# Indexer queries and keys projected features first, with the rotary product on features

## The chip, the cores and the metric

The kernel runs on one core of one Trainium2 chip. The metric is the device time of one execution in microseconds (us). Three runs of the kernel before took 337.05, 338.77 and 338.71 us; the median is 338.71 us.

## What is computed

One encoder layer over 512 tokens with 1024 features. After an RMS norm, one projection feeds two head groups. Group A is attention over 128 keys per query, chosen by a small indexer; group B is latent attention over all admissible keys. Both outputs are gated, concatenated, projected and added to the input. The change touches the indexer's inputs only:

```python
q_i = q_i.reshape(B, S, IDX_HEADS, IDX_DIM)                    # 8 heads of 64
q_i = concatenate([rope(q_i[..., :32], pos), q_i[..., 32:]], -1)
k_i = k_i[:, :, None, :]                                       # one head of 64
k_i = concatenate([rope(k_i[..., :32], pos), k_i[..., 32:]], -1)[:, :, 0, :]
...
rel   = relu(einsum('bqhd,bsd->bqhs', q_i, k_i))
score = einsum('bqhs,bqh->bqs', rel, w_i) * idx_scale          # then mask, top 128
# rope on 32 features: [x1*cos - x2*sin, x2*cos + x1*sin], x1 the first 16, x2 the last 16
```

The first 128 queries need no choice (they have at most 128 keys), so the indexer runs for the token tiles 1, 2 and 3 (384 queries).

## The kernel before

Nearly all products are made of three matmuls on values split into a high and a low part (`mm3`, `mm3w`: high by high, high by low, low by high). Weights arrive in chunks of 128 rows by DMA into `wst`; ScalarE (ACT) rounds a chunk to its high part `wh`, and GpSimd (POOL), or for some chunks VectorE (DVE), subtracts to get the low part `wl`. Chunks 0 to 7 are those of `q_i`, 8 to 15 of `c_kv`, 16 to 23 of `c_q` (whose low parts DVE makes). There are three `wst` buffers for chunks from 8 on, and nine each of `wh` and `wl`, so a chunk waits until TensorE (PE) is through with the chunk nine places ahead.

The order on PE is the order in which the program is written; the helpers `stream` and `weave` interleave several accumulations, and `later` puts a piece of work off by a stated time. The other engines take the order that the scheduler chose when the kernel was built, strictly one after another. PSUM has eight banks in four tags: `mm` 3, `tr` 2, `sc` 2, `pv` 1.

The stretch in question lies from about 15 to 58 us:

- The "small" projection (104 columns: key rope of group B, indexer key, indexer weights) accumulates with features on partitions. Its last eight matmuls use the low weights `swl`. Then `use_small` copies it out, transposes it by token (four 104-wide transposes into `tr`), rotates the key on DVE, and transposes it back to features (`turn2`), where ACT rounds it to KIH and DVE subtracts to KIL.
- The queries: for each of three token tiles, eight steps of three matmuls with 512 columns (72 matmuls), tokens on partitions, in the banks `mm`, `mm`, `pv`. The three accumulations start 1.99 steps apart. `use_qi` copies and rotates (DVE multiplies by tables `cs32` broadcast over heads), then four transposes per tile bring features on partitions, ACT writes the high parts into `QI[0]` and `QI[1]`, and DVE the low parts beside them.
- The `c_kv` projection follows: two accumulations (banks `mm` and `pv`) of eight steps each, the second starting three steps after the first. After nine steps the indexer is woven in: for each tile (3, 2, 1) and head, two matmuls into the banks `sc` and `tr` in turn, a ReLU on ACT in place, and one multiply-add on DVE into `acc`. With two banks a tag, head 4 needs the bank that head 0 used, once DVE has added head 0. The `c_q` projection is woven between the later heads.
- On POOL, between the `wl` subtractions, lie the tables `tb` and `ta` for the rotary products of the other heads.

Of the kernel before, what the change touches and what calls it, by code (L numbers as in the profile page):

```python
# [15 lines left out]
S = 512  # L16
# [9 lines left out]
def constants():  # L26

    pos = np.arange(S, dtype=np.float32)

    def table(d):  # L30
        half = d // 2
        freqs = np.power(10000.0, -np.arange(half) * 2.0 / d).astype(np.float32)
        ang = (pos[:, None] * freqs[None, :]).astype(np.float64)
        c, s = np.cos(ang), np.sin(ang)
        t = np.stack([np.concatenate([c, c], 1), np.concatenate([-s, s], 1)], 1)
        return t.reshape(NT, 128, 2, d).transpose(1, 2, 0, 3).reshape(128, -1).astype(np.float32)

    q = np.arange(128)
    mask = np.where((q[None, :] // 64) <= (q[:, None] // 64), 0.0, NEG).astype(np.float32)
    wide = np.concatenate([np.zeros((128, 384), np.float32), mask], 1)  # L40
    return np.ascontiguousarray(
        np.concatenate([table(64), table(32), np.eye(128, dtype=np.float32), wide], 1))

# [17 lines left out]
KEEP_UP = 4  # L63

WARM = 11

TK = (2, 5, 5, 13, 12, 6)
I0, I1, I2 = 9, 5, 20
# [20 lines left out]
def layer(ctx: ExitStack, tc: tile.TileContext, x, norm_gain, w_in, a_q_norm, a_k_norm, b_q_latent,  # L89
# [14 lines left out]
    def tmp(shape=(128, 512)):  # L104
        return sb("tmp", shape)
# [5 lines left out]
    def psum(tag):  # L111
        return PS.tile([128, 512], F32, name=tag, tag=tag, bufs=BANKS[tag])

    def f32(ap):
        return ap.bitcast(F32)
# [4 lines left out]
    def tok(t):  # L120
        return slice(t * 128, t * 128 + 128)
# [11 lines left out]
    def transpose(o, i, idn):  # L133
        nc.tensor.transpose(o, i, idn)  # L134
        clock[0] += 107.0

    def later(ns, fn, served=False):

        waiting.append((clock[0] + ns, len(waiting), fn, served))
# [72 lines left out]
        nc.sync.dma_start(xin[t // 2][:, t % 2], xv[:, t])  # L212
    for a in range(0, 8, 4):
        ks = slice(a, a + 4)
        nc.sync.dma_start(wst[:, ks, 0:32], wv[:, ks, 3272:3304])
        nc.sync.dma_start(wst[:, ks, 32:104], wv[:, ks, 2560:2632])


    nc.gpsimd.memset(ident, 1.0)
# [12 lines left out]
    def after(v, u):  # L232

        tc.add_manual_dep(v.ins, u.ins.name, mybir.DependencyInfo(
            mybir.DependencyClass.NoSync, mybir.DependencyReason.DATA), reason="order")
# [9 lines left out]
    for _ in range(WARM):  # L245
        matmul(warm, zero[:, 0:128].bitcast(F32R), zero.bitcast(F32R), True, True)

    wake = P.tile([128, 1], F32, name="wake")
    wake_ = nc.scalar.activation(wake, epsc, AF.Square)
    for d in (nc.scalar.dma_start(grow[0:8], norm_gain.rearrange("(k p) -> k p", p=128)),  # L250
# [4 lines left out]
    def first(ins, m):  # L255

        for c in copies[used[0] + 1 + m:]:
            after(c, ins)
# [61 lines left out]
    def tok_jobs(name, nk, lh, ll, n, tiles, use, c=0, mm3=mm3):  # L320

        def job(t):
            def step(a, k):
                h, l = wt(name, k)
                mm3(a[:, :n], lh(k)[:, tok(t)], ll(k)[:, tok(t)], h[:, c:c + n], l[:, c:c + n], k == 0, k == nk - 1)
            return nk, step, lambda a: use(t, a)

        return [job(t) for t in tiles]
# [33 lines left out]
    def xh(k):  # L362
        return XH[k // 4][:, k % 4]
# [69 lines left out]
    def halves(ap):  # L433
        return ap.rearrange("p h (s d) -> p h s d", s=2)
# [9 lines left out]
    def split(h, l, p):  # L444
        return nc.scalar.copy(h, p), nc.vector.tensor_tensor(l, p, f32(h), op=OP.subtract)  # L445


    sm = P.tile([128, NT, 104], F32, name="sm")
    KIH = sb("z3", (128, S), F32R, "kih")
    KIL = sb("z3", (128, S), F32R, "kil")  # L450

    QSUM = []

    def use_small(_, a):
        st = tmp()
        first(nc.scalar.copy(st[:104], a[:104]), KEEP_SMALL)

        def turn():
            p = psum("tr")
            for t in range(NT):  # L460
                transpose(p[:, t * 104:t * 104 + 104], st[:104, tok(t)], ident[:104, :104])
            nc.scalar.copy(sm.rearrange("p t c -> p (t c)"), p[:, :416])
            p3 = p[:, :416].rearrange("p (t c) -> p t c", t=NT)

            kid = tmp((128, NT, 128))
            k4 = kid.rearrange("p t (u d) -> p t u d", u=2)
            m = tmp((128, NT, 32))
            for u in range(2):
                nc.scalar.copy(k4[:, :, u, 32:64], p3[:, :, 64:96])
            src = p3[:, :, 32:64]  # L470
            nc.vector.tensor_tensor(halves(m), halves(src)[:, :, ::-1, :], halves(cs32[:, 1]), op=OP.mult)
            nc.vector.tensor_tensor(src, src, cs32[:, 0], op=OP.mult)
            for u in range(2):
                nc.vector.tensor_tensor(k4[:, :, u, 0:32], src, m, op=OP.add)
            nc.scalar.activation(sm[:, :, 96:104], sm[:, :, 96:104], AF.Copy, scale=512 ** -0.5)

            def turn2():
                p = psum("tr")
                for t in range(NT):
                    transpose(p[:, tok(t)], kid[:, t], ident)  # L480
                kil = split(KIH, KIL, p)[1]
                if len(QSUM) == 3:
                    after(kil, QSUM[2])
            later(LAG_KI, turn2)
        later(LAG_SMALL, turn)

    dve = [None]
# [19 lines left out]

    def lat_kv(_, a):
        latent(a, 11, ckv, ckvs, "pt2")

    x_turn(0)
    gp = psum("sc")
# [21 lines left out]
    for a in range(0, 8, 4):  # L534
        ks = slice(a, a + 4)
        SWD.append(nc.vector.tensor_tensor(SWL[:, ks], wst[:, ks], f32(SWH[:, ks]), op=OP.subtract))
    qi_ = stream(tok_jobs("q_i", 8, xh, xl, 512, [1, 2, 3], lambda t, a: use_qi(t, a), mm3=mm3w), 3, ("mm", "mm", "pv"), 1.99)
    for i, ks in enumerate(((0,), (1,), (2, 3), (4, 5), (6, 7))):
        for k in ks:
            small_step(1, k)  # L540
        run(take(qi_, i // 2 + 1))
        if i == 0:
            xa, xd = [[f[hf, k] for hf in range(2) for k in range(8)] for f in (XA, XD)]
            chain(wake_, SQ[0], SQ[1], SQ[2], gains_, *xa[:2], SQ[3], SWA[0], *xa[2:8], copies[0],
                  *xa[8:10], copies[1], *xa[10:12], copies[2], *xa[12:], copies[3], copies[4])
            chain(TTR[0], TTR[1], *SCL[0], *SCL[1], TTR[2], TTR[3], xd[0], *SCL[2], *xd[1:], dsubs[0], *SWD)
            chain(*POW[0], *POW[1], *POW[2], *POW[3], *SCL[3], SWA[1], *subs[:3])
        if i == 2:
            nc.sync.dma_start(cs32, cst[:, 512:768])
    for k in range(8):  # L550
        matmul(sm_acc[:104], SWL[:, k], xh(k), False, k == 7)
    nc.sync.dma_start(wide, cst[:, 896:1408])
# [8 lines left out]
    HALF = slice(0, 64), slice(64, 128)  # L561
    QI = [sb("qk8", (128, 4, 384), F32R, f"qi{u}") for u in range(2)]

    def use_qi(t, a):
        q = tmp()
        q3 = q.rearrange("p (h d) -> p h d", h=8)
        m = tmp((128, 8, 32))
        a3 = a.rearrange("p (h d) -> p h d", h=8)
        first(nc.scalar.copy(q3[:, :, 32:64], a3[:, :, 32:64]), KEEP_QI)
        rope_mul(a3[:, :, 0:32], m, a3[:, :, 0:32], cs32, t, 8, 32)  # L570
        QSUM.append(nc.vector.tensor_tensor(q3[:, :, 0:32], a3[:, :, 0:32], m, op=OP.add))

        def turn():
            p = psum("tr" if t == 1 else "sc")
            for h in range(4):
                transpose(p[:, tok(h)], q[:, tok(h)], ident)
            p3 = p.rearrange("p (h c) -> p h c", h=4)
            for u in range(2):
                nc.scalar.copy(QI[u][HALF[u], :, tok(t - 1)], p3[HALF[u]])
            for u in range(2):  # L580
                a, b = QI[u][HALF[u], :, tok(t - 1)], QI[u][HALF[1 - u], :, tok(t - 1)]
                nc.vector.tensor_tensor(b, p3[HALF[u]], f32(a), op=OP.subtract)
        later(LAG_QI, turn)

    run(qi_)
    with tc.issue_after(subs[-1].ins):
# [6 lines left out]
    def index():  # L593
        for t in (3, 2, 1):
            n = (t + 1) * 128
            acc = masks[t] = ACC[t]
            for h in range(8):
                u = h % 2
                p = psum(("sc", "tr")[h % 2])
                matmul(p[:, :n], QI[u][:, h // 2, tok(t - 1)], KIH[:, :n], True, False)  # L600
                matmul(p[:, :n], QI[u][:, h // 2, tok(t - 1)], KIL[:, :n], False, True)
                r = p
                nc.scalar.activation(r[:, :n], p[:, :n], AF.Relu)
                w = sm[:, t, 96 + h:97 + h]
                if h == 0:
                    nc.vector.scalar_tensor_tensor(acc, r[:, :n], w, wide[:, 512 - n:], op0=OP.mult, op1=OP.add)
                else:
                    dve[0] = nc.vector.scalar_tensor_tensor(acc, r[:, :n], w, acc, op0=OP.mult, op1=OP.add).ins
                yield 1
# [69 lines left out]

    sq = tmp((128, 2, NT, 32))  # L680
    ssr = small(4)
    src = sm[:, :, 0:32]
    nc.scalar.activation(sq[:, 0], src, AF.Square)
    nc.vector.tensor_reduce(ssr, sq[:, 0], axis=AX.X, op=OP.add)
    nc.vector.tensor_scalar(kb, ssr, 1.0 / 96, EPS, op0=OP.mult, op1=OP.add)
# [382 lines left out]
```

## Time and profile before

| what | value |
|---|---|
| runs | 337.05, 338.77, 338.71 us |
| median | 338.71 us |
| profiled execution: span from the first to the last instruction | 335.4 us |
| the median less that span | 3.3 us |
| granted TensorE clock, mean | 0.999 |
| mean DMA traffic over the span | 104 GB/s |

The page gives no time for the profiled execution other than its span; the 3.3 us are what lies around it (and what one execution differs from another). The page lists busy time by engine, then the chain of work that ended last, then groups of instructions. A busy PE is not PE at its peak, since the ends of matmuls are modelled: rows of PE overlap, and what counts is the distance between the starts of two neighbours. A row of the timeline gives start, duration, engine, line, operation, output and inputs, shapes, and a count where several were merged; in brackets stands the idle time before it and what ended it.

### The profile page before, as it was taken

The page shows a single profiled execution, that of the slowest core. Times are in us where ns is not written, and L with a number is a line of the kernel's source. Part 1 is how long each engine was busy: PE and PEld are TensorE (multiplying, and loading weights), DVE is VectorE, ACT ScalarE, POOL GpSimd, SP SyncE. Part 2 cuts the span into 40 slices and gives each one's busy share as a digit, 9 for nine tenths or more (in the row PEclk, how much of TensorE's full clock was granted, in tenths as well). Part 3 has the DMA queues.
Part 4 walks back from the last instruction along what each step waited for, and adds up shares of the span by engine and source line. Part 5 has one row for each costly group of instructions (what it writes and reads, how often), then busy time and mean ns, then how long its engine had stood idle before and what let it go on. Part 6 is the DMA issues. An engine that isn't in the chain of part 4 may idle for free.

```text
span 335.4 us, 5485 instructions
## 1 busy us (share of the span) xinstructions
PE 327.5 (98%) x1691; PEld 274.0 (82%) x1691; DVE 261.3 (78%) x630; ACT 214.8 (64%) x530; POOL 183.7 (55%) x203
## 2 busy tenths in 40 slices
PE   7799999999999999999999999999999999999995
PEld 5788887888898988888888888888788788888884
DVE  4863779769999595778899989777997776878466
ACT  3935659583666676878876889434526988978210
POOL 3756443366899996235714579538734535745100
PEclk9999999999999999999999999999999999999999
DMA  7932343233133325014200354307977324410006
GB/s 254 306 108 51 108 119 117 63 104 95 34 103 94 94 70 150 1 34 122 70 30 1 73 144 136 91 0 183 241 173 225 96 74 141 127 64 1 2 0 250
DMA packets 28663, 34.77 MB, mean 104 GB/s; under 512 B 5325, under 2 KB 16730, under 8 KB 28634
## 3 DMA queue, kind: packets, MB, share of 16 engines
q1 hardware_dynamic: 25856, 32.45, 33.8%
q10 hardware_dynamic: 2778, 1.97, 2.2%
q8 instruction: 13, 0.21, 0.3%
q14 instruction: 16, 0.13, 0.1%
HBM read 27.07 MB, written 2.10 MB: 87 GB/s over the span
## 4 chain that ended last, share of the span: by engine, by line
PE 91%; DVE 3%; DMA 2%; issue 1%; ACT 1%; POOL 1%; SPq 0%; DVEq 0%; POOLq 0%
PE mm L130 53%; PE sc L130 12%; PE pv L130 11%; PE tr L134 6%; PE tr L130 5%; DMA xin<-in_x 2%; PE mm L134 2%; DVE ob L1023 2%; PE sc L134 1%; PE pv L134 1%; POOL tmp L838 0%; SPq L212 0%; DVE mal L841 0%; DVE z L762 0%; DVE xin L383 0%
## 5 line engine op out<-in xcount | busy, mean ns | idle before, releaser
L300 POOL TENSOR_TENSOR wl<-wst,wh 128x512 fp32r<-128x512 f32 (+2 forms) x80 | 100.6, 1267 | 47.8 <-ACT wh L297 38.6
L297 ACT CAST wh<-wst 128x512 fp32r<-128x512 f32 (+2 forms) x89 | 50.7, 587 | 23.5 <-DMA wst<-in_w_in 12.3
L130 PE MATMUL mm<-wh,xh 128*128 128x512 f32 x112 | 47.0, 419 | 0.0
L130 PE MATMUL mm<-wl,xh 128*128 128x512 f32 x112 | 44.4, 396 | 0.0
L130 PE MATMUL mm<-wh,xl 128*128 128x512 f32 x112 | 44.3, 395 | 0.0
L764 ACT ACTIVATE z<-z,sml 128x256 f32<-128x256 f32 (+2 forms) x64 | 35.9, 561 | 10.0 <-DVE sml L762 9.2
L793 POOL TENSOR_SCALAR z<-z,sml 128x512 f32<-128x512 f32 (+2 forms) x32 | 18.0, 564 | 42.4 <-DVE sml L789 32.8
L227 POOL TENSOR_TENSOR sml<-sml,nhalf 128x4 f32<-128x4 f32 (+2 forms) x28 | 31.8, 1141 | 14.9 <-ACT sml L916 13.7
L130 PE MATMUL mm<-xh,wh 128*128 128x512 f32 x88 | 36.6, 416 | 0.0
L130 PE MATMUL mm<-xl,wh 128*128 128x512 f32 x88 | 34.8, 395 | 0.0
L130 PE MATMUL mm<-xh,wl 128*128 128x512 f32 x88 | 34.7, 394 | 0.0
L619 DVE MAX8 m<-acc 128x8 f32<-128x512 f32 (+2 forms) x48 | 26.4, 553 | 0.0
L620 DVE MATCH_REPLACE8 acc<-m,acc 128x512 f32<-128x512 f32 (+2 forms) x48 | 26.0, 543 | 0.0
L130 PEld LDWEIGHTS mm<-wh,xl 128*128 128x128 f32 x112 | 21.1, 188 | 4.8
L130 PEld LDWEIGHTS mm<-wl,xh 128*128 128x128 f32 x112 | 21.2, 189 | 3.4 <-POOL wl L300 0.4
L130 PEld LDWEIGHTS mm<-wh,xh 128*128 128x128 f32 x112 | 21.1, 189 | 3.0 <-issue 0.2
L445 DVE TENSOR_TENSOR pl<-tr,ph 128x512 fp32r<-128x512 f32 (+1 forms) x32 | 17.6, 548 | 4.7 <-ACT ph L445 4.7
L762 DVE CUSTOM_DVE_ANT_0 z<-sc,wide,nqb 128x512 f32<-128x512 f32 (+3 forms) x32 | 17.3, 542 | 4.3 <-PE sc L130 4.0
L445 ACT CAST ph<-tr 128x512 fp32r<-128x512 f32 (+1 forms) x32 | 15.1, 473 | 8.5 <-PE tr L134 8.1
L130 PE MATMUL sc<-kl,bhl 96*128 96x512 f32 (+3 forms) x96 | 20.0, 320 | 0.0
L130 PEld LDWEIGHTS mm<-xh,wl 128*128 128x128 f32 x88 | 16.5, 188 | 3.9
L130 PEld LDWEIGHTS sc<-kl,bhl 96*128 96x128 f32 x96 | 16.7, 189 | 3.0
(248 smaller groups left out, 879.2 us busy)
## 6 DMA issues: line engine op xcount, KB each, us to landing
wst<-in_w_in SPq DMA_DIRECT2D x48, 256.0 KB, 2.7
wst<-in_w_out SPq DMA_DIRECT2D x16, 256.0 KB, 2.8
xin<-in_x SPq DMA_DIRECT2D x4, 512.0 KB, 5.5
ob<-in_x SPq DMA_DIRECT2D x8, 256.0 KB, 3.5
wst<-in_w_in SPq DMA_DIRECT2D x8, 192.0 KB, 2.4
wst<-in_w_uq SPq DMA_DIRECT2D x6, 192.0 KB, 2.5
wst<-in_w_in SPq DMA_DIRECT2D x8, 128.0 KB, 2.2
wst<-in_w_ukv SPq DMA_DIRECT2D x4, 256.0 KB, 2.9
```

What stands on the lines that cost most here:

```text
L130: nc.tensor.matmul(o, l, r, start=start, stop=stop)
L134: nc.tensor.transpose(o, i, idn)
L227: return nc.gpsimd.tensor_tensor(dst, src, nhalf[:, :src.shape[-1]], op=OP.pow)
L297: copies.append(nc.scalar.copy(h, st))
L300: i = E(eng).tensor_tensor(l, st, f32(h), op=OP.subtract)
L445: return nc.scalar.copy(h, p), nc.vector.tensor_tensor(l, p, f32(h), op=OP.subtract)
L619: nc.vector.max(m, masks[t])
L620: MR.append(nc.vector.match_replace(masks[t], m, masks[t], -3e38))
L762: m = nc.vector.tensor_tensor_reduce(z, sc[:, :n], mask(t), nq(h, t), 3e38, OP.add, OP.min, r[:, i:i + 1])
L764: e = nc.scalar.activation(z, z, AF.Exp, bias=r[:, i:i + 1], scale=-1.0, accum_out=r[:, 2 + i:3 + i])
L793: nc.gpsimd.tensor_scalar(z, z, w, 0.0, op0=OP.mult, op1=OP.add)
L1023: ADD[name, c, t] = nc.vector.tensor_tensor(o, p[:, :n], o, op=OP.add)
```

## The change

The queries are now projected with features on partitions: four groups of 128 features (two heads each), the weight chunk as the stationary operand and the 384 tokens of tiles 1 to 3 as the moving one. That is 32 steps of three matmuls with 384 columns (96 matmuls), in the banks `mm`, `mm`, `pv`, `sc`, again 1.99 steps apart. The small projection's columns are put in another order, so that the indexer key lies on partitions 0 to 63. For each group, and for the key, VectorE shuffles the 32 partitions of a quadrant (feature i gets feature i+16 modulo 32) from PSUM into `bq`, multiplies PSUM by a table of cosines (ones for the features without rotation), GpSimd multiplies the shuffled copy by a table of sines (zeros there), and VectorE adds the two in SBUF. ACT and DVE write high and low parts from that sum. The sixteen 128-wide transposes are gone, the four 104-wide ones are 40 wide. Two tables `turns` (256 KB each) are loaded.

```diff
+    turns = [sb("pt2", (128, S), name=f"turns{i}") for i in range(2)]
...
     def use_small(_, a):
-        st = tmp()
-        first(nc.scalar.copy(st[:104], a[:104]), KEEP_SMALL)
+        st, m = tmp(), tmp()
+        first(nc.scalar.copy(st[64:104], a[64:104]), KEEP_SMALL)
+        w = sb("bq", (64, S))
+        nc.vector.stream_shuffle(w, a[0:64], [(i + 16) % 32 for i in range(32)])
+        nc.vector.tensor_tensor(m[0:64], a[0:64], turns[0][0:64], op=OP.mult)
+        nc.gpsimd.tensor_tensor(w, w, turns[1][0:64], op=OP.mult)
+        nc.vector.tensor_tensor(m[0:64], m[0:64], w, op=OP.add)
+        for u in range(2):
+            nc.scalar.copy(KIH[HALF[u]], m[0:64])
+        for u in range(2):
+            kil = nc.vector.tensor_tensor(KIL[HALF[u]], m[0:64], f32(KIH[0:64]), op=OP.subtract)
...
+    def qi_jobs():
+        def job(g):
+            def step(a, k):
+                h, l = wt("q_i", k)
+                mm3(a[:, :384], h[:, tok(g)], l[:, tok(g)], xh(k)[:, 128:], xl(k)[:, 128:], k == 0, k == 7)
+            return 8, step, lambda a: use_qi(g, a)
+        return [job(g) for g in range(4)]
...
-    qi_ = stream(tok_jobs("q_i", 8, xh, xl, 512, [1, 2, 3], lambda t, a: use_qi(t, a), mm3=mm3w), 3, ("mm", "mm", "pv"), 1.99)
+    qi_ = stream(qi_jobs(), 4, QI_BANK, QI_SKEW)
...
+    def use_qi(g, a):
+        m, w = tmp((128, 384)), sb("bq", (128, 384))
+        p = a[:, :384]
+        nc.vector.stream_shuffle(w, p, [(i + 16) % 32 for i in range(32)])
+        nc.vector.tensor_tensor(m, p, turns[0][:, 128:], op=OP.mult)
+        (nc.gpsimd if QI_POOL else nc.vector).tensor_tensor(w, w, turns[1][:, 128:], op=OP.mult)
+        QSUM.append(nc.vector.tensor_tensor(m, m, w, op=OP.add))
+        for u in range(2):
+            nc.scalar.copy(QI[u][HALF[u], g], m[HALF[u]])
+        for u in range(2):
+            nc.vector.tensor_tensor(QI[u][HALF[1 - u], g], m[HALF[u]], f32(QI[u][HALF[u], g]), op=OP.subtract)
```

The old `use_qi` and the old `turn`, `turn2` of `use_small` go; they stand in the listing of the kernel before.

On VectorE the stretch between the last query rotation and the indexer's first multiply-add (`acc<-sc,sm,wide`) read, in the kernel before:

```order
L439 TENSOR_TENSOR tmp<-pv,cs_142 128x256
L442 TENSOR_TENSOR pv<-pv,cs_142 128x8x32
L571 TENSOR_TENSOR tmp<-pv,tmp 128x8x32
L445 TENSOR_TENSOR kil<-tr,kih 128x512
L582 TENSOR_TENSOR qi_386<-sc,qi_386 64x4x128
L582 TENSOR_TENSOR qi_387<-sc,qi_387 64x4x128
L686 TENSOR_TENSOR kr<-sm,tb_147 128x128
L300 TENSOR_TENSOR wl<-wst,wh 128x384
L582 TENSOR_TENSOR qi_386<-sc,qi_386 64x4x128
L582 TENSOR_TENSOR qi_387<-sc,qi_387 64x4x128
L300 TENSOR_TENSOR wl<-wst,wh 128x384 x3
L606 SCALAR_TENSOR_TENSOR acc_511<-sc,sm,wide 128x512
```

Here `sc`, `tr` and `pv` are PSUM, the rest is SBUF. In the changed kernel the same place, from the shuffle of the third group in `pv` on, reads (the sums and the low parts of the queries now take both inputs from SBUF, and thirteen such rows stand between the last shuffle and `acc`):

```order
L578 STREAM_SHUFFLE bq<-pv 128x384
L579 TENSOR_TENSOR tmp<-pv,turns_98 128x384
L578 STREAM_SHUFFLE bq<-sc 128x384
L579 TENSOR_TENSOR tmp<-sc,turns_98 128x384
L585 TENSOR_TENSOR qi_400<-tmp,qi_400 64x384
L585 TENSOR_TENSOR qi_401<-tmp,qi_401 64x384
L688 TENSOR_TENSOR kr<-sm,tb_149 128x128
L309 TENSOR_TENSOR wl<-wst,wh 128x384 x2
L581 TENSOR_TENSOR tmp<-tmp,bq 128x384 x2
L309 TENSOR_TENSOR wl<-wst,wh 128x384
```

Behind these rows follow four more subtractions `qi<-tmp,qi`, one more `wl`, and then `acc`. Ahead of them, the first two groups are worked off in this order on VectorE:

```order
L475 TENSOR_TENSOR kil<-tmp,kih 64x512 x2
L578 STREAM_SHUFFLE bq<-mm 128x384
L579 TENSOR_TENSOR tmp<-mm,turns_98 128x384
L581 TENSOR_TENSOR tmp<-tmp,bq 128x384
L578 STREAM_SHUFFLE bq<-mm 128x384
L579 TENSOR_TENSOR tmp<-mm,turns_98 128x384
L585 TENSOR_TENSOR qi_400<-tmp,qi_400 64x384
L585 TENSOR_TENSOR qi_401<-tmp,qi_401 64x384
L581 TENSOR_TENSOR tmp<-tmp,bq 128x384
```

So the multiply that frees `pv` stands behind the sums of the first two groups and both low parts of the first. On GpSimd the five products `bq<-bq,turns` come in between the weight subtractions and the tables:

```order
L470 TENSOR_TENSOR bq<-bq,turns_99 64x512
L309 TENSOR_TENSOR wl<-wst,wh 128x256 x4
L580 TENSOR_TENSOR bq<-bq,turns_99 128x384
L309 TENSOR_TENSOR wl<-wst,wh 128x256
L580 TENSOR_TENSOR bq<-bq,turns_99 128x384
L309 TENSOR_TENSOR wl<-wst,wh 128x256 x2
L422 TENSOR_TENSOR tb_148<-cs_144,gb 128x128
```

The last two products stand behind the six `tb` rows and one more `wl`, and ahead of the `ta` rows. On ScalarE the casts of the last two groups (`qi<-tmp`) stand behind the casts of weight chunks 16 to 18. From the indexer's first multiply-add on, the order of every engine is what it was.

More of the change, by code (lines that the diff above doesn't have):

```diff
@@ L40, in constants @@
     wide = np.concatenate([np.zeros((128, 384), np.float32), mask], 1)
+    freqs = np.power(10000.0, -np.arange(16) * 2.0 / 32).astype(np.float32)
+    ang = (pos[None, :] * freqs[:, None]).astype(np.float64)
+    c, s = np.cos(ang), np.sin(ang)
+    head = np.stack([np.concatenate([c, c, np.ones((32, S))]), np.concatenate([-s, s, np.zeros((32, S))])], 1)
+    feat = np.concatenate([head, head]).reshape(128, -1).astype(np.float32)
     return np.ascontiguousarray(
-        np.concatenate([table(64), table(32), np.eye(128, dtype=np.float32), wide], 1))
+        np.concatenate([table(64), table(32), np.eye(128, dtype=np.float32), wide, feat], 1))
 AHEAD = 8
@@ L65 @@
 WARM = 11
+QI_SKEW = 1.99
+QI_BANK = "mm", "mm", "pv", "sc"
+QI_POOL = True
 TK = (2, 5, 5, 13, 12, 6)
@@ L214, in layer @@
         ks = slice(a, a + 4)
-        nc.sync.dma_start(wst[:, ks, 0:32], wv[:, ks, 3272:3304])
-        nc.sync.dma_start(wst[:, ks, 32:104], wv[:, ks, 2560:2632])
+        nc.sync.dma_start(wst[:, ks, 72:104], wv[:, ks, 3272:3304])
+        nc.sync.dma_start(wst[:, ks, 0:72], wv[:, ks, 2560:2632])
     nc.gpsimd.memset(ident, 1.0)
@@ L445, in split @@
         return nc.scalar.copy(h, p), nc.vector.tensor_tensor(l, p, f32(h), op=OP.subtract)
-    sm = P.tile([128, NT, 104], F32, name="sm")
+    sm = P.tile([128, NT, 40], F32, name="sm")
+    HALF = slice(0, 64), slice(64, 128)
     KIH = sb("z3", (128, S), F32R, "kih")
@@ L460, in turn @@
             for t in range(NT):
[L461 to L484, printed above, removed]
+                transpose(p[:, t * 40:t * 40 + 40], st[64:104, tok(t)], ident[64:104, 64:104])
+            p3 = p[:, :160].rearrange("p (t c) -> p t c", t=NT)
+            nc.scalar.copy(sm, p3)
+            nc.scalar.activation(sm[:, :, 0:8], sm[:, :, 0:8], AF.Copy, scale=512 ** -0.5)
         later(LAG_SMALL, turn)
@@ L549, in layer @@
             nc.sync.dma_start(cs32, cst[:, 512:768])
+            for i in range(2):
+                nc.sync.dma_start(turns[i], cst[:, 1408 + i * S:1408 + i * S + S])
     for k in range(8):
@@ L562, in layer @@
     QI = [sb("qk8", (128, 4, 384), F32R, f"qi{u}") for u in range(2)]
[L564 to L583, printed above, removed]
+    def use_qi(g, a):
[9 more added lines that the diff above has]
+            nc.vector.tensor_tensor(QI[u][HALF[1 - u], g], m[HALF[u]], f32(QI[u][HALF[u], g]), op=OP.subtract)
     run(qi_)
@@ L603, in index @@
                 nc.scalar.activation(r[:, :n], p[:, :n], AF.Relu)
-                w = sm[:, t, 96 + h:97 + h]
+                w = sm[:, t, h:h + 1]
                 if h == 0:
@@ L681, in layer @@
     ssr = small(4)
-    src = sm[:, :, 0:32]
+    src = sm[:, :, 8:40]
     nc.scalar.activation(sq[:, 0], src, AF.Square)
```

## Prediction

> **What bounds the kernel now.** I read the page first: busy times, then the chain of work that ended last.
>
> ```profile
> PE 327.5 (98%) x1691; PEld 274.0 (82%) x1691; DVE 261.3 (78%) x630; ACT 214.8 (64%) x530; POOL 183.7 (55%) x203
> ...
> PE 91%; DVE 3%; DMA 2%; issue 1%; ACT 1%; POOL 1%; SPq 0%; DVEq 0%; POOLq 0%
> ```
>
> TensorE is busy for 98% of the span and carries 91% of the chain. So a microsecond of matmul or transpose removed anywhere is a microsecond off the end, and a microsecond for which TensorE waits is one on it, as long as no other engine is late. The next view, busy time by stretch, asks who that could be around the change.
>
> ```profile
> 24.00:32.00 8.00, 8.00 (x38) 6.41 (x37) 2.45 (x5) 3.92 (x11) 4.27 (x5) 1.00 0.19 47
> 32.00:40.00 8.00, 8.00 (x42) 6.47 (x41) 5.26 (x12) 5.02 (x12) 3.11 (x6) 1.00 0.30 77
> 40.00:46.00 6.00, 6.00 (x30) 4.88 (x29) 5.85 (x9) 2.83 (x6) 5.96 (x14) 1.00 0.43 122
> 46.00:58.00 12.00, 12.00 (x54) 9.52 (x53) 9.39 (x16) 9.74 (x20) 2.59 (x2) 1.00 0.45 132
> ```
>
> The columns are PE, weight loads, DVE, ACT, POOL, each with its count. From 24 to 40 us DVE and POOL have room; from 40 to 46 both are full (5.85 and 5.96 of 6.00); from 46 on DVE has 2.6 us to spare in twelve. The change puts its new work on DVE and POOL in just these stretches.
>
> **TensorE's own work.** The timeline gives the distance of starts.
>
> ```profile
> 19.30 0.40 PE L130 MATMUL mm<-wh,xh 128*128 128x512 f32 x1
> 20.70 0.28 PE L130 MATMUL mm<-xh,swh 128*104 128x256 f32 x1
> ...
> 91.01 0.34 PE L130 MATMUL sc<-wh,lath 128*128 128x384 f32 x1
> 92.06 0.39 PE L130 MATMUL mm<-xh,wh 128*128 128x512 f32 x1
> ...
> 27.94 0.52 PE L134 MATMUL tr<-ident,tmp 104*128 104x104 f32 x4
> 28.55 0.40 PE L130 MATMUL mm<-wh,xl 128*128 128x512 f32 x1
> ...
> 35.35 0.60 PE L134 MATMUL tr<-ident,tmp 128*128 128x128 f32 x4
> 36.02 0.40 PE L130 MATMUL pv<-wh,xl 128*128 128x512 f32 x1
> ```
>
> Six 512-column matmuls lie between 19.30 and 20.70: 0.233 us each. Six of 384 columns lie between 91.01 and 92.06: 0.175. The queries cost 72 x 0.233 = 16.8 us before and 96 x 0.175 = 16.8 after: nothing. Four transposes and one matmul lie between 35.35 and 36.02: 0.67 - 0.23 = 0.44 us a set, and four sets go: -1.75. The small set takes 28.55 - 27.94 - 0.23 = 0.38; with 40 columns it takes something between nothing and that, I take 0.25, nearer the row: -0.13. Sum: **-1.9 us**.
>
> Where TensorE then stands:
>
> ```profile
> 23.28 2.00 PE L130 MATMUL mm<-xh,swl 128*104 128x512 f32 x8
> 25.12 0.40 PE L130 MATMUL pv<-wh,xh 128*128 128x512 f32 x1
> ...
> 36.48 0.39 PE L130 MATMUL mm<-xh,wh 128*128 128x512 f32 x1
> 50.12 0.40 PE L130 MATMUL sc<-kih,qi 128*128 128x512 f32 x1
> ...
> 19.29 3.28 DVE L536 TENSOR_TENSOR swl<-smw,swh 128x416 fp32r<-128x416 f32 x2
> ```
>
> Nine query steps stand ahead of the eight `swl` matmuls; a step shrinks from 0.70 to 0.525, so these begin 1.5 us sooner, at 21.8. The second `swl` is ready at 22.57, the fifth matmul wants it at 22.7: just no wait. The small sum ends at 23.7 (25.12 before), the queries at 23.7 + 23 x 0.525 + 0.25 = 36.0 (36.48 before).
>
> **The new wait, and its price.** The price is set by what a DVE instruction costs beside POOL.
>
> ```profile
> 18.69 0.68 DVE L300 TENSOR_TENSOR wl<-wst,wh 128x512 fp32r<-128x512 f32 x1
> 26.97 1.38 DVE L300 TENSOR_TENSOR wl<-wst,wh 128x512 fp32r<-128x512 f32 x1 [4.40 <-ACT wh L297]
> 29.37 0.29 DVE L471 TENSOR_TENSOR tmp<-tr,cs 128x128 f32<-128x128 f32 x1 [1.02 <-ACT tmp L469]
> 42.00 0.91 DVE L686 TENSOR_TENSOR kr<-sm,tb 128x128 f32<-128x128 f32 x1
> 42.83 0.81 DVE L300 TENSOR_TENSOR wl<-wst,wh 128x384 fp32r<-128x384 f32 x1
> 46.65 0.56 DVE L300 TENSOR_TENSOR wl<-wst,wh 128x384 fp32r<-128x384 f32 x1 [0.28 <-ACT wh L297]
> 41.27 0.69 DVE L582 TENSOR_TENSOR qi<-sc,qi 64x512 fp32r<-64x512 f32 x1
> ...
> 41.31 0.75 POOL L300 TENSOR_TENSOR wl<-wst,wh 128x256 fp32r<-128x256 f32 x1
> 42.01 0.75 POOL L413 TENSOR_TENSOR ta<-tmp,ga 128x256 f32<-128x256 f32 x1
> ```
>
> The same subtraction of two SBUF inputs takes 0.68 us alone and 1.38 beside a POOL instruction; `kr` takes 0.91 where a product of its size takes 0.29, and ends 0.15 after the POOL row that began with it; the 384-wide one takes 0.81 against 0.56. But `qi<-sc,qi`, with one input in PSUM, takes 0.69 with a POOL row right across it. So a DVE instruction with both inputs in SBUF waits out the POOL instruction that is under way: 0.70, 0.62 and 0.25 us in these rows. I take 0.4 between POOL's weight and table rows, near the middle. [...]
>
> The change turns the PSUM inputs of the low parts into SBUF ones and adds five sums: fifteen such instructions, and five POOL products. Prices:
>
> ```profile
> 33.21 0.43 DVE L442 TENSOR_TENSOR mm<-mm,cs 128x256 f32<-128x256 f32 x1
> ...
> L300 POOL TENSOR_TENSOR wl<-wst,wh 128x384 fp32r<-128x384 f32 x6 | 6.1, 1027 | 0.4 <-ACT wh L297 0.4
> L500 POOL TENSOR_TENSOR tmp<-tmp 128x512 f32<-128x512 f32 x3 | 3.9, 1298 | 9.5 <-ACT tmp L497 9.5
> ...
> 25.32 0.59 ACT L456 COPY tmp<-mm 104x512 f32<-104x512 f32 x1 [5.95 <-PE mm L130]
> 47.26 0.75 DVE L606 SCALAR_TENSOR_TENSOR acc<-sc,sm,wide 128x512 f32<-128x512 f32 x1
> ```
>
> A POOL product costs 1.0 us (384) or 1.3 (512). A DVE multiply out of PSUM lies between 0.43 (256) and 0.69 (512): 0.55. No row shows a shuffle; below lies 0.43, above 0.91 (the dearest plain row of its kind), and I take a multiply's 0.55 to 0.6 (0.7 for the key), the nearest in width and source. [...]
>
> Now the DVE queue in its order. The key: TensorE's sum is there at 23.9, ACT's copy takes 0.6 (24.6), shuffle and multiply 1.4 (26.0), the `wl` of chunk 7 behind POOL's of chunk 6 1.0 (27.0); POOL's product follows (28.1); the sum behind a `wl` of POOL 29.3; ACT's KIH 30.0; two KIL 31.7. Group 0: shuffle and multiply 32.8, POOL's product 33.7, the sum behind a `wl` 34.8. Group 1: shuffle and multiply 35.9. Then two low parts and a sum, each 0.55 + 0.4: 38.7. Group 2, which holds bank `pv`: shuffle and multiply, **39.9**. TensorE wants `pv` for the second `c_kv` accumulation four steps of 0.70 behind 36.0, at 38.8. **Wait: 1.1 us.**
>
> From 39.9 DVE goes on without a pause: shuffle and multiply of group 3 (41.0); the thirteen two-input rows shown with the change, each 0.47 from start to start (0.2 for `kr`), 5.8 in all; about ten of them meet a POOL row, since POOL still has `wl`, two products and seven `ta` to do: 10 x 0.4 = 4.0. That is 50.7; the first `acc` takes 0.75: **51.4**, where the kernel before has it at 48.0 (47.26 + 0.75). Head 4 of the indexer needs the bank that this frees. It came 50.12 - 36.48 = 13.6 us behind the queries' end; less three transpose sets that go (1.3) and with the 1.1 above, it is wanted at 36.0 + 12.3 + 1.1 = 49.4. **Wait: 2.0 us**, and some 0.2 more until DVE and TensorE are in step: DVE is 3.4 us late there, and up to 58 us it had 2.6 to spare.
>
> Sum: -1.9 + 1.1 + 2.0 + 0.2 = **+1.4 us** on the span of 335.4; what lies around it, 3.3 to the median of the runs, stays. 338.71 + 1.4 = **340.1 us**, +0.4%. Behind 58 us every engine has its old order, so the shift runs through to the end. The two `turns` loads (0.5 MB) cost nothing: they are queued behind the query weights, and the DMA share is 0.19 from 24 to 32 us; if the cover were gone, the first multiply would be late by what the load is late. The lighter ACT and PSUM traffic gains nothing, since neither is waited for here.
>
> **Rivals.**
>
> *The gain comes through whole.* If DVE's two-input rows meet few POOL rows, its queue reaches `acc` at 46 to 47 and neither wait exists: -1.9, 336.8 us. For it speaks the room of both engines between 24 and 40 us; against it `kr` at 0.91 and the 5.96 of 6.00 on POOL.
>
> *Slower, by dearer meetings.* Place: DVE's rows between 35 and 51 us. If each meeting with POOL costs what `kr` shows (0.62 and not 0.4), the 13 counted meetings add 2.9 us: 343.0. A shuffle of 0.91 would add 0.35 x 4 = 1.4 by itself. It is slower by over 0.5% (1.7 us, about what a measurement of this kernel can tell from no change) once a meeting costs over 0.43, so my own figure lies just on this side.
>
> *The change only half does what it says:* the wait for `pv` comes, that for head 4 doesn't, because casts and sums of the last groups slip into gaps: -1.9 + 1.1 = -0.8, 337.9.
>
> **How the numbers follow.** Forecast 0.5, and with its own spread of about 1.2 us either way it lies within 0.5% for 0.3 and above for 0.2. Gain whole 0.2 (0.15 faster by over 0.5%, 0.05 within). Dearer meetings 0.2, all slower. Half 0.1, within. So faster 0.15, within 0.45, slower 0.4. The range goes from the whole gain (336.6) to most of the dearer meetings (342.4); the forecast's own range is 338.9 to 341.3.
>
> **What would show it.** TensorE's first `mm<-xh,wh` with 512 columns at about 36.0 (the -1.9 is on its way); a wait of TensorE in front of the first `pv<-xh,wh` with 512 columns, put down to DVE, of about 1 us; another in front of head 4 (`sc<-kih,qi`), about 2 us; sums and low parts on DVE at 0.9 and more where POOL is busy, 0.55 where it isn't; the shuffle at 0.5 to 0.6. Wrong would be: a shuffle above 0.9, two-input rows of 0.55 beside POOL, no gap on TensorE between 36 and 52 us, or one ahead of 36 (a `wl` of chunk 6 or 7, or `turns`, too late).

## The result, and the profile after

| what | value |
|---|---|
| kernel before, beside the changed one | 337.88 us median (336.56 to 338.78, 6 runs) |
| changed kernel | 341.09 us median (340.08 to 342.12, 6 runs) |
| ratio | 1.0102, 95% interval 1.0072 to 1.0132 |
| span of the profiled execution, before and after | 335.4 and 339.2 us |
| mean granted clock, before and after | 0.999 and 0.994 |

The change makes the kernel slower by 1.0%. The profiled span grows by 3.8 us. The six runs of the kernel before include the three from which the median of 338.71 us came. The page of the changed kernel, in the lines that were read before (busy times, chain, and the granted clock in 40 slices of 8.5 us):

```profile
PE 328.0 (97%) x1699; PEld 277.1 (82%) x1699; DVE 270.6 (80%) x640; ACT 215.3 (63%) x528; POOL 191.9 (57%) x208
PEclk9999997999999999999999999999999999999999
PE 84%; DVE 8%; DMA 3%; issue 2%; POOL 1%; ACT 1%; SPq 0%; DVEq 0%; POOLq 0%; ACTq 0%
```

TensorE carries 84% of the chain and no longer 91%, and DVE has come in with 8%. One slice, the seventh (51 to 59 us), shows a 7 in the clock: that was not there before. The same stretches as before, busy time by engine (PE, weight loads, DVE, ACT, POOL, then clock, DMA share, GB/s):

```profile
24.00:32.00 8.00, 8.00 (x48) 7.70 (x47) 5.63 (x9) 4.78 (x11) 6.08 (x6) 1.00 0.16 39
32.00:40.00 8.00, 7.47 (x39) 6.57 (x38) 7.20 (x14) 3.52 (x9) 6.79 (x10) 1.00 0.36 102
40.00:46.00 6.00, 6.00 (x26) 4.88 (x27) 5.91 (x8) 1.53 (x3) 6.00 (x10) 1.00 0.26 75
46.00:58.00 12.00, 9.30 (x35) 7.17 (x34) 11.84 (x19) 9.56 (x20) 3.37 (x6) 0.86 0.44 125
```

DVE is now full to the end of the stretch (11.84 of 12.00), and TensorE, which was busy throughout, has lost 0.5 us before 40 and 2.7 behind 46. The waits of TensorE between 28 and 70 us and its timeline say where:

```profile
PE sc L138 <- DVE acc L608: 2.7, 1, 2.7
PE pv L138 <- DVE tmp L579: 0.5, 1, 0.5
```

```profile
36.39 0.40 PE L138 MATMUL mm<-xh,wh 128*128 128x512 f32 x1
...
38.97 0.39 PE L138 MATMUL mm<-xh,wl 128*128 128x512 f32 x1
39.89 0.49 PE L138 MATMUL pv<-xh,wh 128*128 128x512 f32 x1 [0.53 <-DVE tmp L579]
40.22 0.40 PE L138 MATMUL pv<-xl,wh 128*128 128x512 f32 x1
...
49.28 0.40 PE L138 MATMUL pv<-xh,wl 128*128 128x512 f32 x1
52.38 0.79 PE L138 MATMUL sc<-kih,qi 128*128 128x512 f32 x1 [2.70 <-DVE acc L608]
52.97 0.63 PE L138 MATMUL sc<-kil,qi 128*128 128x512 f32 x1
53.40 0.63 PE L138 MATMUL pv<-xh,wh 128*128 128x512 f32 x1
...
55.68 0.40 PE L138 MATMUL tr<-kih,qi 128*128 128x512 f32 x1
```

Both predicted waits are there. By the starts, the first costs 39.89 - 38.97 - 0.23 = 0.7 us, and 0.1 more in the matmul behind it; the second 52.38 - 49.28 - 0.23 = 2.9. Then comes something that was not predicted: from 52.38 to 55.68 lie eight steps of 512 columns that take 3.30 us where eight times 0.233 make 1.87. That is 1.4 us more, with no wait between them. The granted clock (the column behind POOL) tells why, in this execution:

```profile
50.00:52.50 2.50, 0.12 (x1) 0.12 (x1) 2.44 (x5) 2.50 (x6) 0.00 (x0) 0.89 0.09 34
52.50:55.50 3.00, 3.00 (x8) 2.38 (x9) 3.00 (x6) 1.39 (x4) 0.00 (x0) 0.53 0.48 131
55.50:58.00 2.50, 2.50 (x13) 2.03 (x12) 2.50 (x5) 2.49 (x6) 0.46 (x1) 1.00 0.66 207
```

TensorE was granted about half its clock (0.53) for the three microseconds behind the long wait, which makes 3.0 x 0.47 = 1.4 us. Head 4 (52.38, and 50.12 before) would stand at 52.38 - 2.9 - 0.8 = 48.7 without the two waits, so TensorE's work became 1.4 us shorter. -1.4 + 0.8 + 2.9 + 1.4 = +3.7 us, against +3.8 in the span: the whole loss lies ahead of 56 us.

### The profile page after: what moved, and what is told of

The parts are those of the page before. It is cut to its first block, busy times and chain, and to the rows that moved or that the text cites. A ratio compares the mean times of both kernels' runs of the same rounds, so it can differ in the third digit from the quotient of the medians.

```text
span 339.2 us, 5519 instructions
## 1 busy us (share of the span) xinstructions
PE 328.0 (97%) x1699; PEld 277.1 (82%) x1699; DVE 270.6 (80%) x640; ACT 215.3 (63%) x528; POOL 191.9 (57%) x208
## 4 chain that ended last, share of the span: by engine, by line
PE 84%; DVE 8%; DMA 3%; issue 2%; POOL 1%; ACT 1%; SPq 0%; DVEq 0%; POOLq 0%; ACTq 0%
PE mm L138 50%; PE sc L138 12%; PE pv L138 8%; PE tr L142 6%; PE tr L138 4%; DMA xin<-in_x 2%; PE mm L142 2%; DVE qi L585 2%; DVE ob L1025 2%; DVE tmp L581 1%; DVE wl L309 1%; PE sc L142 1%; DMA wst<-in_w_in 1%; PE pv L142 1%; POOL wl L309 1%
## 5 line engine op out<-in xcount | busy, mean ns | idle before, releaser
L138 PE MATMUL mm<-xh,wh 128*128 128x512 f32 (+1 forms) x104 | 42.3, 407 | 0.0
L138 PE MATMUL mm<-wh,xh 128*128 128x512 f32 x96 | 40.6, 423 | 0.1
L138 PE MATMUL mm<-xl,wh 128*128 128x512 f32 (+1 forms) x104 | 40.3, 388 | 0.0
L138 PE MATMUL mm<-xh,wl 128*128 128x512 f32 (+1 forms) x104 | 40.3, 387 | 0.0
L138 PE MATMUL mm<-wl,xh 128*128 128x512 f32 x96 | 38.0, 396 | 0.0
L138 PE MATMUL mm<-wh,xl 128*128 128x512 f32 x96 | 37.9, 395 | 0.0
L138 PEld LDWEIGHTS mm<-xh,wl 128*128 128x128 f32 x104 | 19.6, 189 | 4.2 <-POOL wl L309 0.2
L138 PEld LDWEIGHTS mm<-wh,xl 128*128 128x128 f32 x96 | 18.1, 188 | 4.3
L138 PEld LDWEIGHTS mm<-xh,wh 128*128 128x128 f32 x104 | 19.7, 189 | 1.6
L138 PEld LDWEIGHTS mm<-xl,wh 128*128 128x128 f32 x104 | 19.8, 190 | 1.5
```

What stands on the lines that cost most here:

```text
L138: nc.tensor.matmul(o, l, r, start=start, stop=stop)
```

## The experiments

The first theory: operations of VectorE with both inputs in SBUF wait for the POOL operation under way, VectorE's queue falls behind, and TensorE waits for it twice. The rival was that VectorE simply has too many operations now. A second theory says that the long wait itself lowers the clock behind it. The runs with the banks, with POOL's rows, with the sums in PSUM and with twelve filling matmuls share one chip, where the kernel before took 336.84 us (19 runs); the other three share a second one.

### The banks in another order

```diff
-QI_BANK = "mm", "mm", "pv", "sc"
+QI_BANK = "pv", "mm", "sc", "mm"
```

> The changed kernel with the four query groups' banks put as pv, mm, sc, mm, so that the first group, not the third, holds pv. The wait of the first swl matmuls at pv (0.8 us in the changed kernel's trace) should go. Theory (VectorE's queue, held up at its meetings with POOL, sets head 4): head 4 of the last tile is still wanted by TensorE before the first acc is done, acc stays at 52 to 52.5, the wait there grows from 2.9 to about 3.6 us and the end is within 0.4 us of the changed kernel's 341. Rival (the order of the banks does it): the time falls by 0.8 us or more, to about 340.

Measured: 341.17 us, ratio 1.0114 (1.0063 to 1.0165). TensorE's head 4 in the timeline:

```profile
52.13 0.80 PE L138 MATMUL sc<-kih,qi 128*128 128x512 f32 x1 [3.50 <-DVE acc L608]
```

The waits view has no line for `pv` any more; the wait at head 4 has grown from 2.70 to 3.50 us, and head 4 starts 0.25 us sooner, as do the rows of DVE's queue ahead of it (`acc` at 51.33 in place of 51.58). The time is that of the theory, and not the rival's 340. So the first wait costs nothing of its own: whatever TensorE gains ahead of head 4 it loses there, since the end of that wait is set by DVE's queue.

### POOL's table rows moved behind

```diff
     run(qi_)
-    with tc.issue_after(subs[-1].ins):
-        tables()
+    tables_after = subs[-1].ins
...
     tk = topk()
+    with tc.issue_after(tables_after):
+        tables()
```

> The changed kernel with the score tables' rows (seven subtractions on POOL, 0.9 to 1.3 us each) issued behind the top-k's setting up in place of ahead of it. VectorE's instructions, their order and their number stay. Theory (sums and low parts whose inputs both lie in SBUF take 0.3 to 0.7 us more while POOL works): these operations fall from about 1.0 to 0.55 us where the rows stood, the first acc ends 1.5 to 2.5 us sooner (50 to 51 in place of 52.3), the wait at head 4 shrinks from 2.9 to under 1.5 us, and the kernel ends 1.5 to 3 us sooner, at 338 to 339.5. Rival (the mere number of VectorE's operations): sums, low parts and acc as before, 341.

Measured: 337.76 us, ratio 1.0028 (1.0003 to 1.0053), span 335.4. DVE has the same instructions in the same order in both kernels. DVE's timeline in the changed kernel (start, duration, line, operation; x2 and x4 are merged rows, whose duration runs from the first start to the last end):

```profile
40.82 2.35 DVE L585 TENSOR_TENSOR qi<-tmp,qi 64x384 fp32r<-64x384 f32 x2
43.20 1.00 DVE L688 TENSOR_TENSOR kr<-sm,tb 128x128 f32<-128x128 f32 x1
44.12 1.83 DVE L309 TENSOR_TENSOR wl<-wst,wh 128x384 fp32r<-128x384 f32 x2
45.88 1.83 DVE L581 TENSOR_TENSOR tmp<-tmp,bq 128x384 f32<-128x384 f32 x2
47.63 0.81 DVE L309 TENSOR_TENSOR wl<-wst,wh 128x384 fp32r<-128x384 f32 x1
48.47 2.60 DVE L585 TENSOR_TENSOR qi<-tmp,qi 64x384 fp32r<-64x384 f32 x4
51.10 0.56 DVE L309 TENSOR_TENSOR wl<-wst,wh 128x384 fp32r<-128x384 f32 x1
51.58 0.74 DVE L608 SCALAR_TENSOR_TENSOR acc<-sc,sm,wide 128x512 f32<-128x512 f32 x1
```

The same view with the rows out of the way:

```profile
40.58 2.35 DVE L585 TENSOR_TENSOR qi<-tmp,qi 64x384 fp32r<-64x384 f32 x2
...
43.88 1.01 DVE L309 TENSOR_TENSOR wl<-wst,wh 128x384 fp32r<-128x384 f32 x2
44.81 1.01 DVE L581 TENSOR_TENSOR tmp<-tmp,bq 128x384 f32<-128x384 f32 x2
...
46.33 2.30 DVE L585 TENSOR_TENSOR qi<-tmp,qi 64x384 fp32r<-64x384 f32 x4
...
49.14 0.75 DVE L607 SCALAR_TENSOR_TENSOR acc<-sc,sm,wide 128x512 f32<-128x512 f32 x1
```

The first pair of low parts, which meets POOL's two products in both kernels, takes 2.35 us in both. Everything that met only a table row before is now at its own pace: pairs of 1.01 in place of 1.83. The six `ta` rows now stand on POOL at 70 to 73 us. `acc` starts 2.4 us sooner. TensorE's wait at head 4 falls to 0.5 us in the waits view, and no slow stretch follows it (the clock is 1.00 in every window from 45 to 58 us). The number of DVE's operations is as before (640 on both pages), so that rival falls. The time is below the 338 to 339.5 that were expected, since the slow stretch went with the wait. By the spans nothing of the loss is left (335.4 in both), by the medians 0.9 us. By the rows, what still holds DVE up is POOL's products and weight rows; this run alone does not show it.

### Product and sum in place in PSUM

```diff
-        m, w = tmp((128, 384)), sb("bq", (128, 384))
-        p = a[:, :384]
+        w = sb("bq", (128, 384))
+        p = m = a[:, :384]
...
-        nc.vector.tensor_tensor(m, p, turns[0][:, 128:], op=OP.mult)
+        nc.vector.tensor_tensor(p, p, turns[0][:, 128:], op=OP.mult)
...
-        QSUM.append(nc.vector.tensor_tensor(m, m, w, op=OP.add))
+        QSUM.append(nc.vector.tensor_tensor(p, p, w, op=OP.add))
```

The same for the key, with the banks `pv`, `mm`, `sc`, `mm`.

> The changed kernel with the product and the sum of the rotary step written in place in the PSUM bank, for keys and queries, and the banks put as pv, mm, sc, mm. VectorE has as many operations as in the changed kernel, but no sum and no low part has both inputs in SBUF any more. Theory (the meetings): sums and low parts take 0.55 to 0.65 us, the wait at head 4 is under 0.5 us, TensorE's saving of 1.9 us comes through: 336 to 337 where the kernel of before has 338. Rival (number of VectorE's operations): acc at 51 to 52.5, 340 to 341. Rival (the bank held until the low part is read): a wait at pv, mm or sc between 36 and 42 us takes the gain, 338 to 340.

Measured: 339.83 us, ratio 1.0059 (1.0032 to 1.0085). The forecast of 336 to 337 missed. Its first half came true. The timelines of POOL, and of DVE behind it, where a sum falls on a POOL row:

```profile
43.33 1.33 POOL L581 TENSOR_TENSOR bq<-bq,turns 128x384 f32<-128x384 f32 x1
44.61 0.46 POOL L424 TENSOR_TENSOR ta<-tmp,ga 128x128 f32<-128x128 f32 x1
45.03 1.11 POOL L309 TENSOR_TENSOR wl<-wst,wh 128x256 fp32r<-128x256 f32 x1
46.10 1.01 POOL L581 TENSOR_TENSOR bq<-bq,turns 128x384 f32<-128x384 f32 x1
```

```profile
45.58 0.57 DVE L582 TENSOR_TENSOR sc<-sc,bq 128x384 f32<-128x384 f32 x1
...
49.58 0.56 DVE L582 TENSOR_TENSOR mm<-mm,bq 128x384 f32<-128x384 f32 x1
```

The sum `sc<-sc,bq` takes 0.57 us right beside a POOL row. But the last two products, which stood ahead of all six `ta` rows in the changed kernel, now stand on POOL behind five and behind all six of them, at 43.33 and 46.10, and a sum cannot start before its product: the last one comes at 49.58. TensorE waits 1.5 us for a low part and 0.9 for an `acc`. The meeting became a plain wait for POOL's result. The wait for the low part is in kind that of the second rival (a bank of `sc` held until the low part is read), but at 47 to 49 us and not at 36 to 42, since the sum ahead of it is late. That POOL's product would be late was in none of the expectations; the next run tests it.

### Both edits together, and a control

> The two edits together: product and sum of the rotary step in place in the PSUM bank (banks pv, mm, sc, mm), and the score tables' rows issued behind the top-k's setting up. In the run with the bank edit alone the last sums came late because their other factor is made by POOL, which was busy with those rows (5.00 of 5 us from 40 to 45). Theory (it is the meetings of VectorE and POOL, by sharing or by waiting for POOL's result, that cost the gain): TensorE waits under 0.5 us in all for the queries, and its saving of 1.9 us comes through: 1.5 to 2 us below the kernel of before, a ratio of 0.994 to 0.996. Rival (the saving is eaten by the greater number of VectorE's operations): waits at head 4 as in the run with the rows late (0.8 us) or more, a ratio of 1.000 to 1.003.

Measured: **335.58 us**, against 337.31 for the kernel before on the same chip, ratio **0.9942 (0.9923 to 0.9961)**, span 334.0. DVE's timeline:

```profile
42.23 0.57 DVE L582 TENSOR_TENSOR sc<-sc,bq 128x384 f32<-128x384 f32 x1
...
46.72 0.75 DVE L608 SCALAR_TENSOR_TENSOR acc<-sc,sm,wide 128x512 f32<-128x512 f32 x1
```

The sum of the third group stands at 42.2 (45.6 in the run with the sums alone), the last one right behind it, `acc` starts 4.9 us sooner than in the changed kernel, and TensorE has no wait left between 28 and 70 us: the waits view lists none in this stretch. Its saving comes through, 1.4 us in the span and 1.7 in the medians. Some 0.3 of the 1.7 goes with the clock: all nine executions have a mean granted clock of 0.998 or more, while seven of the twenty of the kernel before have 0.995 or less; the other thirteen have a median of 336.99, 1.4 above this version. It has the same 640 operations on DVE as the changed kernel, and it beats both kernels.

The control moves the table rows in the kernel of before, with the edit that moved them in the changed kernel.

> The kernel of before, with the score tables' rows issued behind the top-k's setting up and nothing else. TensorE has no wait behind VectorE between 36 and 58 us in this kernel, so the theory expects nothing of it: a ratio of 0.998 to 1.002, and all that the moved rows bring to the changed kernel is the removal of its own wait. Rival (the rows cost every kernel something, later or elsewhere): 0.5% or more faster.

Measured: 336.79 us, ratio 0.9992 (0.9973 to 1.0011), no difference. The moved rows are worth nothing where DVE is not late. DVE's timeline of the control also shows what `kr` takes with hardly any POOL row beside it, and how soon the next row follows:

```profile
41.71 0.29 DVE L687 TENSOR_TENSOR kr<-sm,tb 128x128 f32<-128x128 f32 x1
41.92 0.55 DVE L300 TENSOR_TENSOR wl<-wst,wh 128x384 fp32r<-128x384 f32 x1
```

### Filling TensorE's wait

Twelve matmuls with zero weights (`blank`) in the wait, to see whether the clock follows the wait or the place:

```diff
...
+                if (t, h) == (3, 4):
+                    for _ in range(12):
+                        matmul(OPEN["pv"], blank, xh(0), False, False)
```

> The changed kernel with twelve more matmuls of 512 columns, with zeros as weights, ahead of head 4 of the last tile, accumulated into a group that is finished (they add nothing). They fill 2.8 us of the 2.9 us in which TensorE waits there. Theory of the clock (TensorE's wait makes the granted clock fall to about 0.5 for the 3 us behind it, which costs 1.4 us): the clock stays at 0.9 or above between 52 and 56 us, the matmuls behind head 4 go at 0.23 us in place of 0.42, and the end is 1 to 1.5 us sooner than the changed kernel's, about 339.7. Rival (the slow matmuls have another cause, the work itself or traffic beside it): they stay at 0.4 us, and the end stays at 341 or later.

Measured: 344.46 us, ratio 1.0209 (1.0164 to 1.0253). The time missed the expected 339.7 by far, but in the profile the clock did as the theory says. The windows (columns as above), and TensorE's timeline at the place where a wait came up instead:

```profile
52.50:55.50 3.00, 3.00 (x14) 2.21 (x13) 3.00 (x6) 1.71 (x5) 0.00 (x0) 1.00 0.40 93
...
62.30:65.50 3.20, 3.15 (x8) 2.77 (x9) 2.64 (x4) 1.05 (x4) 0.05 (x1) 0.50 0.21 77
```

```profile
62.35 0.69 PE L138 MATMUL tr<-kih,qi 128*128 128x384 f32 x1 [2.13 <-DVE acc L616]
```

Head 4 has no wait and the matmuls behind it run at full clock. But a cast on ACT had moved ahead of the latent's copy and waited 1.68 us for its weights; DVE waited for ACT, TensorE for DVE: 2.1 us at 62.35, and behind that wait the clock is 0.50 for three microseconds. The slow stretch went along with the wait, to other matmuls. Most of this kernel's loss is not the clock's, though: one of its four executions took 344.00 us at a mean clock of 0.998.

The second try fills less, so that a shorter wait stays at the old place:

```diff
...
+                    for _ in range(5):
+                        nc.tensor.matmul(OPEN["pv"], blank, xh(0), start=False, stop=False)
```

> The changed kernel with five more matmuls of 512 columns, with zeros as weights, ahead of head 4 of the last tile (they add nothing). They shorten TensorE's wait there from 2.9 to about 1.7 us and leave the place and the end of the wait where they are (52.4 us). Theory of the clock (a wait of 2.3 us and more makes the granted clock fall for 3 us, one of 1.6 us doesn't): no clock below 0.9 from 52.5 to 55.5 us, matmuls at 0.23 us behind head 4, the end 0.8 to 1.4 us sooner than the changed kernel's, as the casts that move beside it take some back or not. Rival (the slow pace belongs to the work at this place): 0.42 us a matmul there as before.

Measured: 340.81 us, ratio 1.0111 (1.0074 to 1.0149), span 338.9. TensorE's timeline:

```profile
52.01 0.51 PE L138 MATMUL sc<-kih,qi 128*128 128x512 f32 x1 [1.55 <-DVE acc L614]
52.35 0.40 PE L138 MATMUL sc<-kil,qi 128*128 128x512 f32 x1
...
59.57 0.45 PE L138 MATMUL tr<-kih,qi 128*128 128x384 f32 x1 [0.92 <-DVE acc L616]
```

The wait is 1.6 us, the windows have the clock at 1.00 from 52.5 to 55.5, and the same matmuls on the same data go at 0.23 us (15 in three microseconds where the changed kernel did 8). The rival (work of this place) falls. That the clock fell or stayed up by chance in these single profiles is not excluded by them (see the last section). In time it brings only 0.3 us of span, where 0.8 to 1.4 were expected: the cast beside it moved again, and TensorE waits at 59.57, 0.9 us by the view and 1.2 by the starts of its matmuls, which takes back most of the 1.4. The two ratios do not tell this kernel from the changed one: that the lowered clock costs 1.4 us is read from the rows, and was not won back in any run by filling the wait alone.

## Why the prediction was right or wrong

The direction and both waits were right, and 341.09 lies in the range. But 340.1 against 338.71 was +0.4%, within what I had called no change as the likeliest outcome, and the result is +1.0%. By the spans it is +1.4 against +3.8 us: the path was right, its size less than half.

That 341.09 came so near to 340.1 is partly luck with the base. In every run whose span is on record, the time is the span plus 1.7 us (1.68 to 1.80). So the profiled execution of the kernel before took about 337.1, and of the 3.3 us that the forecast added, 1.6 were the distance to other executions of the same kernel. From 337.1 the same sum gives 338.5. By steps:

- **TensorE's saving, -1.9: mis-sized.** It was 1.4 (the reading above, and the version without waits). The queries end at 36.39, not 36.0. The `swl` matmuls begin at 21.79 as predicted; the rest is lost in the small transposes and in 384-wide matmuls at 0.177 rather than 0.175:

```profile
26.64 0.34 PE L138 MATMUL mm<-xh,wl 128*128 128x384 f32 x1
26.91 0.44 PE L142 MATMUL tr<-ident,tmp 40*128 40x40 f32 x4
27.27 0.44 PE L138 MATMUL mm<-xh,wh 128*128 128x384 f32 x1
27.56 0.34 PE L138 MATMUL mm<-xl,wh 128*128 128x384 f32 x1
```

From 26.64 to 27.56 stand two matmuls (0.35) and 0.57 us for a set that was put at 0.25; the 104-wide one took 0.38. Narrower transposes saved nothing here.

- **The wait at `pv`: right in mechanism, 0.8 and not 1.1.** DVE's multiply freed the bank at 39.8 (predicted 39.9); TensorE came 0.4 later than thought. The first experiment shows that its size didn't matter in this kernel.
- **The price of a meeting: right.** Predicted were ten meetings at 0.4, 4.0 us, between the last multiply and `acc`. In the rows above, the surplus over the pace without POOL is 1.2 for the first pair (2.35 against 1.15, half of the four that take 2.30), 0.71 for `kr` (1.00 against 0.29 in the control), 0.82 twice, 0.26 and 0.30: 4.1 us in nine rows, 0.46 each. The shuffle too: 0.58 to 0.61, predicted 0.55 to 0.6. The point at which I said it would turn slower by over 0.5% was 0.43, so 0.46 lies just on the other side.
- **The wait at head 4: 2.9 and not 2.0.** TensorE wanted the bank at 49.5 (predicted 49.4), but `acc` ended at 52.3 and not 51.4. The failing term is "each 0.47 from start to start (0.2 for `kr`), 5.8 in all". From 40.82 to 51.58 lie 10.76 us; less the meetings that is 6.7, 0.9 more. The six low parts on 64 partitions follow each other at 0.575 (2.30 for four) and not at 0.47, which is 0.6 of it; 0.47 is the pace of rows on 128 partitions (a pair of 0.55 takes 1.01). The rest lies in rounding and in short gaps where rows of different kinds follow each other. The 0.2 for `kr` was right: in the control the next row follows 0.21 behind it.
- **"Some 0.2 more until DVE and TensorE are in step": wrong in kind.** In its place came 1.4 us of slow matmuls, from the lowered clock. The trace of before had no long wait outside its first 12 us, and I gave a wait no price beyond its length. The 0.2 was also too small by itself: where the clock stayed up (five filling matmuls), DVE's lateness cost TensorE another wait of 1.2 us at 59.57.
- **The rivals.** The gain coming through whole failed as the profile had argued. The half change failed: the wait at head 4 was the larger. Dearer meetings, as a mechanism, did not come: 0.46, not 0.62. The time went a third of the way from 340.1 to that rival's 343.0, for other reasons.

That VectorE's rows with both inputs in SBUF take longer while POOL works, on which the sum of the waits rested, is borne out by the runs: the run with the rows late has the same DVE queue and loses the surplus with the POOL rows (pairs of 1.83 us fall to 1.01), and a sum with one input in PSUM takes 0.57 us beside POOL.

## What to carry to other kernels

Before work is moved from a busy TensorE to VectorE and GpSimd, list which new VectorE operations have both inputs in SBUF and which GpSimd rows they will fall on: here each such meeting cost 0.46 us on average, and keeping product and sum in place in PSUM, with GpSimd's unrelated rows moved behind, turned +1.0% into -0.6%. When two engines are tied by data as well as by meetings, removing the meetings alone was not enough here (+0.6% with product and sum in PSUM and GpSimd's rows left where they were): the product also had to come early in GpSimd's queue (-0.6% with the rows moved as well). And a long wait of TensorE can have a price beyond its length: behind 2.7 us, the lower clock (0.53 for three microseconds) cost another 1.4 us of matmul time in the profiled execution, though not in every execution.

## What the hardware showed that was not expected

In the stretch from 35 to 70 us, waits of 2.1, 2.7 and 3.5 us (the view's figures, with twelve matmuls in the wait, in the changed kernel, and with the banks in another order) were each followed by three microseconds at a granted clock of 0.50, 0.53 and 0.59; waits of 0.5 to 1.6 us, in five kernels, by none.

These are single profiled executions, and the length of the wait does not settle the matter. Three microseconds at 0.53 bring the mean clock of 339 us down to 0.996 at most (the profiled execution has 0.994). Two of the six executions of the changed kernel have a mean of 0.999 and 1.000, and one of the four with the banks in another order has 0.999: these had no such stretch. No trace of them was kept, so whether their wait at head 4 was as long is not shown. The two of the changed kernel have spans of 338.7 and 338.3 us, only 0.5 to 0.9 below the profiled 339.2; so less than the 1.4 us may be left of the slow stretch at the end, as the new wait with five filling matmuls also suggests. The mean clock varies between executions of one kernel (0.994 to 1.000 in the six of the changed one), and what decides it no run shows.

A low clock is also seen at the start of the kernel in some executions and not in others. Behind TensorE's wait for the input at about 11 us, two kernels with that part of the program unchanged (first the product and sum in place, then both edits together) show:

```profile
11.00:13.00 2.00, 1.61 (x9) 1.61 (x9) 2.00 (x6) 2.00 (x7) 1.90 (x3) 0.64 0.92 287
13.00:16.00 3.00, 3.00 (x21) 3.00 (x20) 1.09 (x3) 1.30 (x4) 1.95 (x3) 0.67 1.01 368
```

```profile
11.00:13.00 2.00, 1.66 (x15) 1.66 (x16) 2.00 (x6) 2.00 (x7) 1.90 (x3) 1.00 0.90 291
13.00:16.00 3.00, 3.00 (x27) 2.99 (x26) 2.15 (x6) 2.83 (x7) 2.83 (x4) 1.00 1.01 367
```

TensorE's waits there were 2.2 and 2.0 us. The profile of the kernel with twelve matmuls in the wait has the low clock there too (0.50 from 11 to 13 us, 0.77 from 13 to 16), behind a wait of 1.7 us, while the kernel before kept its clock at 1.00 behind 1.8. Some 1.5 us of the spans with the product and sum in place and with twelve matmuls are owed to this and not to the edits, an estimate from these clocks and TensorE's busy time in the two windows.

It also goes with the spread of about 2 us between times of one kernel. Of the 19 runs of the kernel before on the first chip, fourteen have a mean clock of 0.997 or more and take 336.4 to 338.0 us; the five with 0.995 or less take 338.3 to 338.9. On the second chip it is thirteen with 336.5 to 337.5 and seven with 338.2 to 338.6. That the low clock of these seven and five lies at the start of the kernel is likely, but only profiled executions show the place. The kernel with the product and sum in place takes 337.6 to 338.3 us in its four executions at 0.998 or more, so its forecast of 336 to 337 missed without the clock as well.
